# Three row-count arms of a mixture-of-experts loop: the smallest arm laid next in line and made to hold the whole expert, the larger ones set apart, and the expert's buffers made fixed tiles

## The chip, the cores and the metric

The kernel runs on one core of a Trainium2 chip. The metric is the device time of one execution in microseconds (us).

## What is computed

The program is two transformer blocks over 256 tokens of width 1024. The first block has a mixture-of-experts feed-forward layer: a router gives each token its best 4 of 32 experts, and each expert is a gate-up product, a clamped activation and a down product with its own weights. Cut to that layer, the reference is:

```python
def clamped_swiglu(hdn):
    x_glu = jnp.minimum(hdn[..., :D_EXPERT], SWIGLU_LIMIT)
    x_lin = jnp.clip(hdn[..., D_EXPERT:], -SWIGLU_LIMIT, SWIGLU_LIMIT)
    return x_glu * jax.nn.sigmoid(SWIGLU_ALPHA * x_glu) * (x_lin + 1)

def moe_ffn(h, w_router, b_router, w_gate_up, b_gate_up, w_down, b_down):
    ...
    logits = (xt @ w_router).astype(jnp.float32) + b_router.astype(jnp.float32)
    top_v, top_i = lax.top_k(logits, TOP_K)
    gates = jax.nn.softmax(top_v, axis=-1)
    ...
    counts = jnp.bincount(e_flat, length=N_EXPERTS)
    ...
```

Which expert gets how many rows is known only when the program runs. Everything is in float32.

## The kernel before

Attention, the norms and the router come first (until about 190 us). Then a Python loop writes out the 32 experts one after the other. Nothing loops at run time: each expert has its own instructions, and branches choose among them by its count of rows `n`.

**Three arms.** For each expert `by_rows` is called twice, once for the gate-up part (label `up{e}`) and once for the down part (label `down{e}`). Each call writes `If(n > 32)` with an inner `If(n > 64)`. Over 64 rows the `mid` arm runs (and in its gate-up part a further test, `If(n > 96)` at L1334, leads to `wide`), over 32 rows the `narrow` arm, else the `few` arm, which is the `Else` and so a jump's target. `few` works on 32 rows, `narrow` on 64, `mid` on 64 and then on 32 more. By the lines that ran, with these inputs experts 9, 13 and 20 take `mid`, 0, 3, 4, 6, 11, 12, 19 and 25 `narrow`, the other 21 `few`, and `wide` doesn't run. Each engine runs every branch for itself. L1317 is the test for 32 rows, L1318 that for 64. At the head of an arm a hint for TensorE (PE) names the branch that comes next (`down{e}` or `up{e+1}`) as likely taken.

**What stands around the arms.** Between the two parts stand `combine` (4 matmuls at L1052, which add the previous expert's output rows to the tokens) and `mask` for the next expert (VectorE, DVE). The down part also prepares the next expert: `gather` (L888) and `gather_out`, `slots` (L987, L989), `slots_out`, `turn_x` (L999). It ends with `rows_out`, a copy on ScalarE (ACT, L1044) and a subtract on DVE (L1047). The next expert's gate-up part begins with its bias, two matmuls at L1038 into the PSUM bank `gl`, which the activation of the expert before was read from by DVE. In the `few` arm the gate-up reads are at L1025 (`gate_up`), the turning of the hidden rows at L1093 (`few_T`), the down reads at L1103 (`few_out`).

**The weight stream.** An expert's weights are 12 slabs of 1024 KB, 8 for gate-up and 4 for down. The class `Stream` issues all of them in order on one queue, SyncE's (SP), at L192, into 17 slots of SBUF taken in turn (11 of a tile named `w`, 6 of tiles named `hi`, `hx`, `lo`, `lx`). When `W.done(i)` is called in the program, slab i's slot is handed to the slab 17 places on, whose load then waits, at run time, for PE's semaphore to show that the last read of slab i is done in whichever arm ran. The calls for slabs 0 to 7 of an expert stand after its `up{e}` branch, those for slabs 8 to 11 after its `down{e}` branch. SP's queue is in order: a load that waits holds up all behind it.

**Buffers.** `xT`, `dT` and `gs` of an expert come from a pool with two buffers, `eb`, `d` and `y` from one with one buffer.

Of the kernel before, what the change touches and what calls it, by code (L numbers as in the profile page):

```python
# [8 lines left out]
F32 = mybir.dt.float32  # L9
F32R = mybir.dt.float32r  # L10
# [9 lines left out]
T, D, NE, DFF = 256, 1024, 32, 2816  # L20
# [76 lines left out]
def kernel(tc, a, out, taps=None, stop=None):  # L97
# [3 lines left out]
    def P(n, bufs=1, stack=es, side="right", **k):  # L101
        return stack.enter_context(tc.tile_pool(name=n, bufs=bufs, side=side, **k))
# [778 lines left out]
    def mask_rows(d, t, e):  # L881
        nc.vector.tensor_scalar(d[:, t, :], C["iota2"], pos[:, t, e:e + 1], None, op0=OP.is_equal)
# [50 lines left out]
    pk0 = P("blk2a")  # L933
    ms = ExitStack()
    m1 = P("moe1", 1, ms)
    m2 = P("moe2", 2, ms)
    GN = {}

    def load_gn(i):
# [11 lines left out]

    acc = [two(t, True) for t in range(2)]

    PRE = {}

    def alloc(e):
        PRE[e] = (m2.tile([128, 4, 128], F32, name="xT"), m2.tile([128, 2, 128], F32R, name="dT"),
                  m1.tile([128, 3, 128], F32R, name="eb"), m2.tile([128, 1], F32, name="gs"))

    banks = {n: one(i) for i, n in enumerate(("ga", "gp", "gl", "li"))}  # L960

# [8 lines left out]
                                C["d32"][:, e:e + 1], None, op0=OP.mult)  # L970

    def mask(e):
        d = m1.tile([128, 2, 128], F32, name="d")
        for t in range(2):
            mask_rows(d, t, e)
        slab_rows(e)
        return d

    def gather_out(b):
        xe = m1.tile([128, 512], F32, name="xe")  # L980
# [68 lines left out]
    def combine(y, dT):  # L1049
        for t in range(2):  # L1050
            for hf in range(2):
                nc.tensor.matmul(acc[t][:, hf * 512:hf * 512 + 512], dT[:, t, :], y[:, hf, :], start=False,  # L1052
                                 stop=False, skip_group_check=True)

    def few_up(e):

        xT, dT, eb, gs = PRE[e]
        b = bank("gl")
        bias(b, eb[:, 1, :], 0)
        bias(b, eb[:, 2, :], 512, False)  # L1060
        nc.vector.tensor_copy(gs[32:64], gs[0:32])
        for o in (0, 64):
            nc.vector.tensor_copy(dT[o + 32:o + 64], dT[o:o + 32].bitcast(F32))
        for k in range(8):
            gate_up((b,), xT, W.get(MOE0 + 12 * e + k), k, 32)
# [41 lines left out]
    def narrow_up(e):  # L1107

        xT, eb = PRE[e][0], PRE[e][2][:, 0, :]
        gl, li = bank("gl"), bank("li")  # L1110
        bias(gl, eb, 0)
        bias(li, eb, 512)
        for k in range(8):
            gate_up((gl, li), xT, W.get(MOE0 + 12 * e + k), k, 64)
# [31 lines left out]
    def mid_up(e):  # L1146

        xT, (eb, *eg) = PRE[e][0], (PRE[e][2][:, q, :] for q in range(3))
        base = MOE0 + 12 * e
        d = m1.tile([128, 2, 128], F32, name="d")  # L1150
        for t in range(2):
            nc.vector.tensor_scalar(d[:, t, :], C["iota4"], pos[:, t, e:e + 1], None, op0=OP.is_equal)
        gl, li = bank("gl"), bank("li")
        bias(gl, eb, 0)
        bias(li, eb, 512)
        gx = bank("ga")
        for t in range(2):
            for q in range(4):
                nc.tensor.matmul(gx[32 * q:32 * q + 32, 0:256], d[:, t, 32 * q:32 * q + 32],
                                 h2[:, t, q * 256:q * 256 + 256], start=(t == 0), stop=(t == 1),  # L1160
                                 skip_group_check=True, tile_position=(0, 32 * q))
        gp = bank("gp")
        for t in range(2):
            nc.tensor.transpose(gp[:, t * 128:(t + 1) * 128], d[:, t, :], ident)
        for t in range(2):
            nc.tensor.matmul(gp[:, 256:257], d[:, t, :], gate[:, t, e:e + 1], start=(t == 0), stop=(t == 1),
                             skip_group_check=True)
        xe = m1.tile([128, 512], F32, name="xe")
        nc.scalar.activation(xe[:, 0:256], gx[:, 0:256], AF.Copy)
        nc.vector.tensor_copy(gs2, gp[:, 256:257])  # L1170
        for hf in range(2):
            nc.vector.tensor_scalar(dT2[:, hf], gp[:, 0:256].rearrange("p (t i) -> p t i", t=2),
                                    C["hm"][:, hf:hf + 1], None, op0=OP.mult)
        gate_up((gl, li), xT, W.get(base), 0, 64)
        gt = bank("ga")
        for c in range(2):
            nc.tensor.transpose(gt[:, c * 128:(c + 1) * 128], xe[:, c * 128:(c + 1) * 128], ident)
        xT2 = m1.tile([128, 2, 128], F32, name="xT2")
        nc.scalar.activation(xT2, gt[:, 0:256].rearrange("p (c s) -> p c s", c=2), AF.Copy)
        gate_up((gl, li), xT, W.get(base + 1), 1, 64)  # L1180
        b2 = bank("ga")
        bias(b2, eg[0], 0)
        bias(b2, eg[1], 512, False)
        for k in range(2, 10):
            if k < 8:
                gate_up((gl, li), xT, W.get(base + k), k, 64)
            gate_up((b2,), xT2, W.get(base + k - 2), k - 2, 32)
# [37 lines left out]
    def wide(e, c0):  # L1225

        base = MOE0 + 12 * e
        d = m1.tile([128, 2, 128], F32, name="d")
        pc = m1.tile([128, 2], F32, name="pc")
        sel = m1.tile([128, 2], F32R, name="sel")  # L1230
        nc.vector.tensor_scalar(pc, pos[:, :, e], float(-c0), None, op0=OP.add)
# [53 lines left out]
                    nc.tensor.matmul(acc[t][:, hf * 512:hf * 512 + 512], dT[:, t, :], y[:, q, :], start=False,  # L1285
                                     stop=False, skip_group_check=True)

    alloc(0)
    slab_rows(0)
    slots(0, d0, banks["gp"])  # L1290
    xe = gather_out(banks["ga"])
# [12 lines left out]
                nc.tensor.matmul(acc[t][:, HV[hf]], gT[:, t * 128:(t + 1) * 128], bd[:, HV[hf]], start=True,  # L1304
                                 stop=False, skip_group_check=True)

    y = None
    bias_down()
    W.done(BIAS)

    def by_rows(n, label, ahead, wide_too, mid, narrow, few):

        def hint():
            if ahead:
                tc.mark_branch_hint_location(ahead, "LikelyTaken", [mybir.EngineType.PE])

        with tc.If(n > 32, label=label) as cmp:  # L1317
            with tc.If(n > 64) as many:  # L1318
                hint()
                if wide_too:  # L1320
                    wide_too()
                mid()
            with many.Else():
                hint()
                narrow()
        with cmp.Else():
            hint()
            few()

    for e in range(NE):  # L1330
        n = nc.values_load(cnt[0:1, e:e + 1], min_val=0, max_val=T)  # L1331

        def more():
            with tc.If(n > 96):  # L1334
                wide(e, 96)
                with tc.If(n > 224):
                    wide(e, 224)

        by_rows(n, f"up{e}", f"down{e}", more, lambda: mid_up(e), lambda: narrow_up(e), lambda: few_up(e))
        for k in range(8):  # L1340
            W.done(MOE0 + 12 * e + k)
        if e:
            combine(y, PRE[e - 1][1])
        if e == 1:
            early_loads()
        d = None
        if e + 1 < NE:
            alloc(e + 1)
            d = mask(e + 1)
        y = m1.tile([128, 2, 512], F32R, name="y")  # L1350
        by_rows(n, f"down{e}", f"up{e + 1}" if e + 1 < NE else None, None, lambda: mid_down(e, d, y),
                lambda: narrow_down(e, d, y), lambda: few_down(e, d, y))
        for k in range(8, 12):
            W.done(MOE0 + 12 * e + k)
    combine(y, PRE[NE - 1][1])

    ms.close()
    rb_stack.close()
# [602 lines left out]
```

## Time and profile before

| | us |
|---|---|
| median of 3 runs | 2109.08 |
| lowest and highest of them | 2105.88 and 2111.14 |
| the profiled execution, its own time | 2107.37 |
| its span in the profile | 2105.6 |
| PE busy in the span | 1810.1 |
| DVE busy | 941.3 |
| ACT busy | 674.9 |

The span is what the profiler saw of the program; the profiled execution's own time is 1.77 us more. Busy times are sums over stages with different limits, so a share of the whole span says little about the expert stage, which lies between about 203 and 1225 us. The names PEld and PEq stand for PE's weight loads and PE's sequencer, the part that takes instructions, waits and branches.

### The profile page before, as it was taken

The numbers are of one execution on the slowest core, as the hardware profiler recorded it, in microseconds if no ns is written. First come the engines' busy times: TensorE is split into PE (matmuls) and PEld (weight loads), VectorE is DVE, ScalarE is ACT, GpSimd is POOL, SyncE is SP. The second block draws the span as 40 slices with busy tenths as digits, with TensorE's granted clock in tenths as the row PEclk, the third lists the DMA queues.
The fourth block names the chain that finished last, engine by engine and source line by source line (L and its number), as shares of the span: only waits on it lengthen the run. The fifth ranks groups of instructions, "written<-read, shape, count | busy, mean of one in ns | idle before, by whom it ended". The sixth has DMA issues, their size and how long they took to land.

```text
span 2105.6 us, 28938 instructions
## 1 busy us (share of the span) xinstructions
PE 1810.1 (86%) x11311; PEld 1160.3 (55%) x11311; DVE 941.3 (45%) x1687; ACT 674.9 (32%) x1149; POOL 365.5 (17%) x337
## 2 busy tenths in 40 slices
PE   7998878876878777877877778999999989999998
PEld 4775223322222222222212158998998778988996
DVE  3763222212112221122112159956576579665763
ACT  3452111101111111011101055544564456545752
POOL 3333000000000000000000034214352233132640
PEclk9997999988998998989878789999999999999999
DMA  9868999997986999899999954445455544453552
GB/s 399 344 250 303 404 413 415 414 412 322 399 326 259 410 413 415 348 388 413 413 414 413 398 173 135 142 175 185 151 182 212 179 132 142 169 194 136 179 195 87
DMA packets 102215, 603.00 MB, mean 286 GB/s; under 512 B 9888, under 2 KB 10576, under 8 KB 47024
## 3 DMA queue, kind: packets, MB, share of 16 engines
q1 hardware_dynamic: 97984, 586.72, 71.3%
q0 software_dynamic: 3952, 12.53, 1.9%
q8 instruction: 179, 2.93, 0.6%
q14 instruction: 100, 0.82, 0.1%
HBM read 598.13 MB, written 1.08 MB: 285 GB/s over the span
## 4 chain that ended last, share of the span: by engine, by line
issue 50%; PE 35%; DVE 9%; POOL 2%; ACT 2%; POOLq 1%; DMA 0%; DVEq 0%; SPq 0%; ACTq 0%
PE psum L354 11%; PE psum L353 10%; PE psum L352 10%; DVE lo L325 1%; DVE lx L325 1%; POOL v L245 1%; DVE gl L1732 1%; DVE gl L1516 1%; DVE h L577 1%; PE psum L1666 0%; DVE x L285 0%; PE psum L448 0%; POOLq L1331 0%; ACT hTh L357 0%; PE psum L416 0%
## 5 line engine op out<-in xcount | busy, mean ns | idle before, releaser
L1025 PE MATMUL psum<-w,xT 128*32 128x512 f32 (+1 forms) x1504 | 265.2, 682 | 26.1 <-DMA w<-in_wgu_dram 24.5
L354 PE MATMUL psum<-hTh,lo 128*128 128x256 f32 x848 | 240.6, 284 | 2.6 <-DVE lo L325 2.6
L352 PE MATMUL psum<-hTh,hi 128*128 128x256 f32 x848 | 242.2, 286 | 0.4 <-DVE yl L1536 0.4
L353 PE MATMUL psum<-hTl,hi 128*128 128x256 f32 x848 | 240.5, 284 | 0.0
L248 POOL TENSOR_TENSOR yr<-v,mhalf 128x1 f32<-128x1 f32 (+1 forms) x26 | 21.0, 808 | 1164.6 <-DVE v L245 1163.3
L325 DVE TENSOR_TENSOR lo<-w,hi 128x2048 fp32r<-128x2048 f32 x84 | 193.7, 2309 | 59.2 <-ACT hi L319 59.2
L319 ACT ACTIVATE hi<-w 128x2048 fp32r<-128x2048 f32 x93 | 177.6, 1913 | 86.4 <-PE psum L354 51.2
L1007 DVE TENSOR_SCALAR g<-psum 64x256 f32<-64x256 f32 (+1 forms) x70 | 29.3, 418 | 364.9 <-PE psum L1025 364.2
L1025 PEld LDWEIGHTS psum<-w,xT 128*32 128x32 f32 (+1 forms) x1504 | 64.5, 129 | 206.4 <-issue 143.4
L1008 ACT ACTIVATE s<-g 64x256 f32<-64x256 f32 (+1 forms) x70 | 28.8, 411 | 452.8 <-DVE g L1007 452.8
L352 PEld LDWEIGHTS psum<-hTh,hi 128*128 128x128 f32 x848 | 162.7, 192 | 3.7 <-issue 3.0
L354 PEld LDWEIGHTS psum<-hTh,lo 128*128 128x128 f32 x848 | 162.4, 192 | 2.8 <-DVE lo L325 2.8
L353 PEld LDWEIGHTS psum<-hTl,hi 128*128 128x128 f32 x848 | 162.4, 191 | 0.0
L1047 DVE TENSOR_TENSOR y<-psum,y 64x512 fp32r<-64x512 f32 x64 | 44.1, 689 | 209.5 <-ACTq L1317 124.5
L1778 POOL TENSOR_TENSOR cv<-cv,cv 128x256 f32<-128x256 f32 x44 | 86.3, 1960 | 135.5 <-ACT cv L1777 129.7
L1038 PE MATMUL psum<-bgh,eb 128*128 128x512 f32 x70 | 32.7, 557 | 87.0 <-issue 72.6
L354 PE MATMUL psum<-hTh,lx 128*128 128x256 f32 x368 | 104.1, 283 | 2.7 <-DVE lx L325 2.7
L352 PE MATMUL psum<-hTh,hx 128*128 128x256 f32 x368 | 104.4, 284 | 0.0
L325 DVE TENSOR_TENSOR lx<-w,hx 128x2048 fp32r<-128x2048 f32 x40 | 92.4, 2310 | 26.3 <-ACT hx L319 26.2
L353 PE MATMUL psum<-hTl,hx 128*128 128x256 f32 x368 | 103.9, 282 | 0.0
L888 PE MATMUL psum<-h,d 128*64 128x512 f32 x248 | 73.2, 700 | 35.3 <-DVE l L1010 16.5
L1772 DVE SCALAR_TENSOR_TENSOR cv<-psum,cols,cv 128x255 f32<-128x255 f32 x176 | 72.8, 475 | 62.3 <-ACT cv L1768 62.3
(427 smaller groups left out, 3774.3 us busy)
## 6 DMA issues: line engine op xcount, KB each, us to landing
w<-in_wgu_dram SPq DMA_DIRECT2D x169, 1024.0 KB, 19.8
w<-in_wpk_dram SPq DMA_DIRECT2D x168, 1024.0 KB, 5.0
w<-in_wd_dram SPq DMA_DIRECT2D x83, 1024.0 KB, 20.1
lo<-in_wgu_dram SPq DMA_DIRECT2D x29, 1024.0 KB, 20.1
hi<-in_wgu_dram SPq DMA_DIRECT2D x28, 1024.0 KB, 18.9
hi<-in_wd_dram SPq DMA_DIRECT2D x16, 1024.0 KB, 20.8
lo<-in_wd_dram SPq DMA_DIRECT2D x15, 1024.0 KB, 20.8
hx<-in_wgu_dram SPq DMA_DIRECT2D x15, 1024.0 KB, 20.1
```

The source lines that it names most:

```text
L319: nc.scalar.activation(s.his[i], W.get(i), AF.Copy)
L325: (eng or nc.vector).tensor_tensor(s.los[i], W.get(i), s.his[i].bitcast(F32), OP.subtract)
L352: nc.tensor.matmul(o, lh, rh, start=start, stop=False, **k)
L353: nc.tensor.matmul(o, lh, rl, start=False, stop=False, **k)
L354: nc.tensor.matmul(o, ll, rh, start=False, stop=stop, **k)
L888: nc.tensor.matmul(b[64 * j:64 * j + 64, :], d[:, t, 64 * j:64 * j + 64], h2[:, t, j * 512:j * 512 + 512], start=(t == 0), stop=(t == 1), ...
L1007: nc.vector.tensor_scalar(g, gl[:, c], 7.0, None, op0=OP.min)
L1025: nc.tensor.matmul(b[o:o + n, :], l, w[:, q * 512:q * 512 + 512], start=False, stop=(k == 7), skip_group_check=True, tile_position=(0, o))
L1038: nc.tensor.matmul(b, lhsT, bgh[:, o:o + 512], start=first, stop=False, skip_group_check=True)
L1047: nc.vector.tensor_tensor(y[o, hf, :], yb[r, :], y[r, hf, :].bitcast(F32), OP.subtract)
L1772: nc.vector.scalar_tensor_tensor(cv[q][:, o], bnk[:, q, i], c4[q][:, 2 * d:2 * d + 1], cv[q][:, o], op0=OP.mult, op1=OP.add)
L1778: nc.gpsimd.tensor_tensor(cv[0], cv[0], cv[1], OP.mult)
```

## The change

The test for 32 rows gets a flag that makes its false side, the `few` arm, the block that comes next in line (`preferred_fallthrough_block=False`), and the tests for 64 and 96 rows get the same flag. The `few` arm now holds the whole expert in the branch `up{e}`: gate-up, `combine` of the previous expert, `mask` for the next one, down part. The branch `down{e}` has no `Else` any more: an expert of at most 32 rows passes it by. `combine` and `mask` have gone from between the two branches into each arm. In the arms for more rows the gate-up part hints `down{e}`, and the down part `up{e+1}`; the `few` arm hints `up{e+1}`. The calls of `W.done` stay where they were, behind the two branches. `xT`, `dT`, `gs` become two fixed tiles each, taken in turn, and `EB`, `dm` and `Y` one fixed tile each, so the count of buffers is the same.

```diff
@@ -933,7 +933,6 @@
     pk0 = P("blk2a")
     ms = ExitStack()
     m1 = P("moe1", 1, ms)
-    m2 = P("moe2", 2, ms)
     GN = {}
 
     def load_gn(i):
@@ -951,11 +950,13 @@
 
     acc = [two(t, True) for t in range(2)]
 
-    PRE = {}
-
-    def alloc(e):
-        PRE[e] = (m2.tile([128, 4, 128], F32, name="xT"), m2.tile([128, 2, 128], F32R, name="dT"),
-                  m1.tile([128, 3, 128], F32R, name="eb"), m2.tile([128, 1], F32, name="gs"))
+
+    ROWS = [(m1.tile([128, 4, 128], F32, name=f"xT{i}"), m1.tile([128, 2, 128], F32R, name=f"dT{i}"),
+             m1.tile([128, 1], F32, name=f"gs{i}")) for i in range(2)]
+    EB = m1.tile([128, 3, 128], F32R, name="eb")
+    PRE = [(ROWS[e % 2][0], ROWS[e % 2][1], EB, ROWS[e % 2][2]) for e in range(NE)]
+    dm = m1.tile([128, 2, 128], F32, name="d")
+    Y = m1.tile([128, 2, 512], F32R, name="y")
 
     banks = {n: one(i) for i, n in enumerate(("ga", "gp", "gl", "li"))}
 
@@ -970,11 +971,9 @@
                                 C["d32"][:, e:e + 1], None, op0=OP.mult)
 
     def mask(e):
-        d = m1.tile([128, 2, 128], F32, name="d")
         for t in range(2):
-            mask_rows(d, t, e)
+            mask_rows(dm, t, e)
         slab_rows(e)
-        return d
 
     def gather_out(b):
         xe = m1.tile([128, 512], F32, name="xe")
@@ -1147,7 +1146,7 @@
 
         xT, (eb, *eg) = PRE[e][0], (PRE[e][2][:, q, :] for q in range(3))
         base = MOE0 + 12 * e
-        d = m1.tile([128, 2, 128], F32, name="d")
+        d = dm
         for t in range(2):
             nc.vector.tensor_scalar(d[:, t, :], C["iota4"], pos[:, t, e:e + 1], None, op0=OP.is_equal)
         gl, li = bank("gl"), bank("li")
@@ -1225,7 +1224,7 @@
     def wide(e, c0):
 
         base = MOE0 + 12 * e
-        d = m1.tile([128, 2, 128], F32, name="d")
+        d = dm
         pc = m1.tile([128, 2], F32, name="pc")
         sel = m1.tile([128, 2], F32R, name="sel")
         nc.vector.tensor_scalar(pc, pos[:, :, e], float(-c0), None, op0=OP.add)
@@ -1285,7 +1284,6 @@
                     nc.tensor.matmul(acc[t][:, hf * 512:hf * 512 + 512], dT[:, t, :], y[:, q, :], start=False,
                                      stop=False, skip_group_check=True)
 
-    alloc(0)
     slab_rows(0)
     slots(0, d0, banks["gp"])
     xe = gather_out(banks["ga"])
@@ -1304,55 +1302,62 @@
                 nc.tensor.matmul(acc[t][:, HV[hf]], gT[:, t * 128:(t + 1) * 128], bd[:, HV[hf]], start=True,
                                  stop=False, skip_group_check=True)
 
-    y = None
     bias_down()
     W.done(BIAS)
 
-    def by_rows(n, label, ahead, wide_too, mid, narrow, few):
-
-        def hint():
-            if ahead:
-                tc.mark_branch_hint_location(ahead, "LikelyTaken", [mybir.EngineType.PE])
-
-        with tc.If(n > 32, label=label) as cmp:
-            with tc.If(n > 64) as many:
-                hint()
-                if wide_too:
-                    wide_too()
+    def first_part(up, e):
+
+        up(e)
+        if e:
+            combine(Y, PRE[e - 1][1])
+        if e + 1 < NE:
+            mask(e + 1)
+
+    def second_part(down, e):
+        down(e, dm if e + 1 < NE else None, Y)
+
+    def arm(n, label, mid, narrow, few=None, ahead=None):
+
+        def hint(l):
+            if l:
+                tc.mark_branch_hint_location(l, "LikelyTaken", [mybir.EngineType.PE])
+
+        with tc.If(n > 32, label=label, preferred_fallthrough_block=False) as cmp:
+            with tc.If(n > 64, preferred_fallthrough_block=False) as many:
+                hint(ahead[0])
                 mid()
             with many.Else():
-                hint()
+                hint(ahead[0])
                 narrow()
-        with cmp.Else():
-            hint()
-            few()
+        if few:
+            with cmp.Else():
+                hint(ahead[1])
+                few()
 
     for e in range(NE):
         n = nc.values_load(cnt[0:1, e:e + 1], min_val=0, max_val=T)
-
-        def more():
-            with tc.If(n > 96):
+        after = f"up{e + 1}" if e + 1 < NE else None
+
+        def mid_first():
+            with tc.If(n > 96, preferred_fallthrough_block=False):
                 wide(e, 96)
                 with tc.If(n > 224):
                     wide(e, 224)
-
-        by_rows(n, f"up{e}", f"down{e}", more, lambda: mid_up(e), lambda: narrow_up(e), lambda: few_up(e))
+            first_part(mid_up, e)
+
+        def few():
+            first_part(few_up, e)
+            second_part(few_down, e)
+
+        arm(n, f"up{e}", mid_first, lambda: first_part(narrow_up, e), few, (f"down{e}", after))
         for k in range(8):
             W.done(MOE0 + 12 * e + k)
-        if e:
-            combine(y, PRE[e - 1][1])
         if e == 1:
             early_loads()
-        d = None
-        if e + 1 < NE:
-            alloc(e + 1)
-            d = mask(e + 1)
-        y = m1.tile([128, 2, 512], F32R, name="y")
-        by_rows(n, f"down{e}", f"up{e + 1}" if e + 1 < NE else None, None, lambda: mid_down(e, d, y),
-                lambda: narrow_down(e, d, y), lambda: few_down(e, d, y))
+        arm(n, f"down{e}", lambda: second_part(mid_down, e), lambda: second_part(narrow_down, e), None, (after, after))
         for k in range(8, 12):
             W.done(MOE0 + 12 * e + k)
-    combine(y, PRE[NE - 1][1])
+    combine(Y, PRE[NE - 1][1])
 
     ms.close()
     rb_stack.close()
```

## Rows read from the trace of the kernel before

**Rows 1.** The page: slices of the span, and the gate-up loads (issue to landing).

```profile
GB/s 399 344 250 303 404 413 415 414 412 322 399 326 259 410 413 415 348 388 413 413 414 413 398 173 135 142 175 185 151 182 212 179 132 142 169 194 136 179 195 87
...
w<-in_wgu_dram SPq DMA_DIRECT2D x169, 1024.0 KB, 19.8
```

**Rows 2.** Windows of the expert stage; last columns clock, DMA share, GB/s.

```profile
203.00:1205.00 1002.00, 787.21 (x4310) 260.66 (x4306) 219.62 (x574) 125.03 (x270) 0.00 (x0) 0.89 0.96 389
615.00:635.00 20.00, 15.87 (x84) 5.09 (x84) 3.19 (x9) 1.22 (x3) 0.00 (x0) 0.91 0.34 127
660.00:685.00 25.00, 19.65 (x124) 7.79 (x124) 4.04 (x11) 2.64 (x5) 0.00 (x0) 0.80 0.61 220
685.00:880.00 195.00, 152.01 (x860) 50.11 (x852) 43.10 (x114) 24.22 (x53) 0.00 (x0) 0.89 1.01 412
```

**Rows 3.** PE's waits in the expert stage: total us, times, longest.

```profile
PE psum L1038 <- issue: 72.6, 25, 5.1
...
PE psum L888 <- DVE l L1010: 16.5, 7, 3.2
PE psum L1038 <- PEq L1334: 14.4, 3, 5.5
```

**Rows 4.** PE's waits from expert 9 to the start of expert 14.

```profile
PE psum L1038 <- issue: 10.5, 4, 4.2
PE psum L1038 <- PEq L1334: 10.4, 2, 5.5
PE psum L888 <- issue: 7.3, 1, 7.3
```

**Rows 5.** PE's waits from expert 20 to the start of expert 22.

```profile
PE psum L1038 <- PEq L1334: 4.0, 1, 4.0
PE psum L1038 <- issue: 2.8, 1, 2.8
```

**Rows 6.** Branches at L1317: ns min/median/max.

```profile
L1317 DVEq COMPARE_BRANCH  x64: 43/56/60, 193.7 to 1182.9; - x64
L1317 PEldq COMPARE_BRANCH  x64: 74/600/6554, 194.1 to 1199.9; - x64
```

**Rows 7.** The same in the last six experts.

```profile
L1317 PEldq COMPARE_BRANCH  x12: 350/840/6235, 1025.7 to 1199.9; - x12
```

**Rows 8.** The test for 96 rows at L1334.

```profile
L1334 PEldq COMPARE_BRANCH  x3: 6187/6226/7053, 448.8 to 834.1; - x3
...
L1334 PEldq EVENT_SEMAPHORE  x3: 51/51/51, 455.0 to 840.3; - x3
```

**Rows 9.** Timeline of PE in expert 13, gate-up reads, first and last.

```profile
622.89 1.94 PE L1025 MATMUL psum<-w,xT 128*64 128x512 f32 x8
...
645.58 1.04 PE L1025 MATMUL psum<-hi,xT 128*32 128x512 f32 x8
```

**Rows 10.** Timeline of SP's loads, experts 13 and 14.

```profile
638.23 3.19 SPq L192 DMA_DIRECT2D w<-in_wgu_dram  x3
...
646.68 0.34 SPq L192 DMA_DIRECT2D hi<-in_wgu_dram  x1
...
674.78 0.89 SPq L192 DMA_DIRECT2D hx<-in_wgu_dram  x1
680.00 0.34 SPq L192 DMA_DIRECT2D lx<-in_wgu_dram  x1
...
686.27 2.27 SPq L192 DMA_DIRECT2D w<-in_wgu_dram  x1
```

**Rows 11.** Timeline of PE in expert 14.

```profile
676.85 1.22 PE L1038 MATMUL psum<-bgh,eb 128*128 128x512 f32 x2 [2.10 <-issue]
...
686.13 1.19 PE L1052 MATMUL psum<-y,dT 128*128 128x512 f32 x4
```

**Rows 12.** Timeline of ACT at the end of expert 14.

```profile
697.16 1.21 ACT L1044 ACTIVATE y<-psum 64x512 fp32r<-64x512 f32 x2 [2.07 <-PE psum L1103]
```

**Rows 13.** Timeline of DVE at the end of expert 14.

```profile
698.40 1.41 DVE L1047 TENSOR_TENSOR y<-psum,y 64x512 fp32r<-64x512 f32 x2 [5.91 <-ACTq L1317]
```

## The prediction, made before the changed kernel was run

> **What bounds the kernel now.** I read the slices of the page first, then windows over the expert stage, PE's waits in it, single branches, and last the order of loads and reads around one large expert.
>
> In the expert stage the DMA stands at 412 to 415 GB/s for most slices, and a load takes 19.8 us from issue to landing while a slab alone takes 1024 KB / 412 GB/s = 2.55 us: some eight loads share the wire, which is full [rows 1]. Twelve slabs are 30.5 us an expert, and in the stretch without a dip PE is busy 152 of 195 us and waits for slabs [rows 2]. A faster arm changes nothing there. Over 203 to 1205 us the mean is 389 GB/s [rows 2], so 1002 x (1 - 389/412) = 56 us is all that the stage can win. That loss lies in dips behind the experts with over 64 rows (9, 13, 20): the wire falls to 127 and 220 GB/s around expert 13 [rows 2]. There PE is late, all 17 slots are full, and the stream stands until PE has read. So there are two kinds of time: most of the stage, where PE's stalls are free, and the run-ups from expert 9 to the start of 14 and from 20 to the start of 22, where each us on PE is a us of the whole.
>
> PE's stalls of the stage sum high: 72.6 us of "issue" ahead of the bias and 14.4 us behind the test for 96 rows [rows 3]. Only the run-ups' part counts: 10.5 + 10.4 + 7.3 = 28.2 [rows 4] and 4.0 + 2.8 = 6.8 [rows 5], together **35.0 us**.
>
> **The change, part by part.**
>
> *The skip of `wide`.* PE's branch at L1334 took 6.2 us each time, and 14.4 us of it showed as idle time, 4.8 each, the rest being covered by work already queued [rows 3, 8]. With the false side in line this goes: -14.4.
>
> *The jump into `narrow`'s and `mid`'s arms.* By the flag the false side of the test for 64 rows comes next too. So `narrow` loses an unhinted jump: the 7.3 us of idle time ahead of a gather are one such fetch, in a run-up [rows 4]: -7.3. `mid` gains two unhinted jumps. That in its gate-up part stands where the skip of `wide` stood, just as close behind the start: 3 x 4.8 = +14.4. That in its down part stands ahead of a gather at which PE waits for DVE in any case, 16.5/7 = 2.4 us [rows 3]; an average shown stall is 72.6/25 = 2.9 us [rows 3], so 3 x (2.9 - 2.4) = +1.5. Bounds: nothing for either, if a jump is short enough to find its target loaded; 3 x 7.3 each if none is covered [rows 4].
>
> *Jumps out and back for more than 32 rows.* The jump out is hinted, and hinted branches in the last six experts mostly took 0.35 to 0.84 us [rows 7], inside the time PE's queue covers: 0. The jump back at the end of an arm has no hint. The down arm's is in the waits of before (the true arms jump over `few`, and the next start waited 2.10 us [rows 11]): these waits I leave as they are. The gate-up arm's was short of that: six experts of the run-ups (9, 11, 12, 13, 19, 20) by 2.9 less 2.4 of DVE's wait, 6 x 0.5 = +3.0. Bounds: 0 and 6 x 2.9 = 17.4.
>
> *`few` holding the whole expert.* PE loses the branches between its parts. They matter in one expert of the run-ups alone, 10, and hardly show there: 0. Before, hints reached the `few` jump; in line it needs none.
>
> *The new wait.* An engine that passes `down{e}` by must top up its semaphore for the work that it didn't do there, as at L1334 [rows 8], and it does so only when it comes to that branch, behind its own work. The next bias waits for DVE to have read its bank; DVE comes to the top-up behind ACT's copy and its own subtract at the end of `rows_out`, 1.21 + 1.41 = 2.6 us after PE's last matmul [rows 12, 13]. What is queued behind the bias is all gate-up reads, and so the slots. In the run-ups that is once (expert 10): +2.6; elsewhere slabs are late anyway. Bounds: 0 and 2.6.
>
> The run-ups then sum to -14.4 - 7.3 + 14.4 + 1.5 + 0 + 3.0 + 2.6 = **-0.2 us**: what it saves on the skip of `wide` it pays in other jumps.
>
> *Slots that come free later.* This is the part that I weigh most. A load waits for one value of PE's semaphore, whichever arm ran, so an arm's reads must lie at a fixed distance from its end. The rows show it: in expert 13 the gate-up reads run from 622.89 to 646.6 [rows 9], but its eight slots are handed on between 638.23 and 646.68, over the last reads, not as the first slabs are done [rows 10]. In `few` of expert 14 it is different: the reads begin at 678.0, behind the bias of 676.85 [rows 11], and the loads for their slots go out from 680.00 to 686.27, one after each slab [rows 10], because the gate-up reads are the last thing in that arm. In the changed kernel the arm goes on through `combine`, `gather`, `slots`, `turn_x` and the down part, while in the other arms the gate-up reads are still the last but `combine`. The value that means "slab 0 read" is then reached, in `few`, some thirty counted matmul groups before its end: slab 0's slot comes free only once `combine` is done, at 686.13 + 1.19 = 687.3 [rows 11], not at 680.0 [rows 10], 7.3 us later, and the next ones in the course of the gather and the down part.
>
> On a full wire with free slots ahead that costs nothing: later slabs are still waited for. It costs where `few` follows a long arm, as the wire is then empty: the last load before 680.00 goes out at 674.78 [rows 10], 5.2 us earlier, twice a slab's time, and the wire was down at 220 GB/s [rows 2]. So the stream starts 7.3 us later, less 2.1 us if the stall at the start of expert 14 goes [rows 11]: 5.2 to 7.3; I take 5.5, since loads already out cover little. That holds for experts 14 and 21 (behind 13 and 20): 11.0. Expert 10, behind 9, is followed by a run-up in which PE sets the time: 0. Expert 1 follows `narrow` with the stream just begun: 0 to 7.3, I take 4. Sum **+15.0 us**. What is queued behind the late load: all loads of the queue, in order, and so expert 15's and 22's reads. Bounds: 0 (the wire not yet empty, or slots counted otherwise) and 4 x 7.3 = 29.
>
> *Fixed tiles.* As many buffers as before, so no wait moves: 0. DVE's and ACT's branches take 0.06 us [rows 6], so what they gain or lose in branches is 0.
>
> Sum: 2107.4 (the profiled execution's own time) - 0.2 + 15.0 = **2122 us**. That execution lies 1.7 us below the median, inside the three runs, so I don't correct for it.
>
> [...] PE's branch at L1317 took from 0.07 to 6.55 us, DVE's 0.06 [rows 6]. [...]
>
> **The rivals.**
>
> *A: the run-ups' stalls all go* (the jump to `mid` lands in what is loaded or is covered, and the ways back too). 35.0 us go, the new wait brings 2.6, the late slots 15.0: 2107.4 - 17.4 = 2090 us. For it: all of these stalls are fetches, and hints work where they stand early [rows 7]. Against it: the way back and the test for 64 rows have none. It decides from the point where the run-ups lose over 15 us, about half their stalls.
>
> *B: no change.* The late slots cost nothing (or as much as the stalls save): 2107.4 - 0.2 = 2107 us, within 6. For it: the loads that the large expert's down part frees may bridge the gap. Against it: 220 GB/s [rows 2].
>
> *C: every jump out and back pays.* The six ways back of the gate-up arms at 2.9 in place of 0.5 (+14.4) and the three jumps into `mid`'s down arm at 2.9 in place of 0.5 (+7.2), on top of the forecast: 2122 + 22 = 2144 us. For it: 6.2 us three times out of three for an unhinted branch [rows 8].
>
> **How the numbers follow.** Forecast 0.44, A 0.27, B 0.14, C 0.15. A measurement of this kernel can tell 0.3%, about 6.3 us. The forecast's own range is 2112 to 2132: its terms with bounds, late slots from 5 to 25. The range for 8 in 10 reaches from A to just past C, 2089 to 2146; it leaves out half of A's lower side and C's upper. Faster is A, 0.27; the same is B and a little, 0.15; slower the rest, 0.58.
>
> **What would show it.** Right: in expert 14 the first load after 675 us goes out after `combine`, not after the first gate-up reads, and the dip behind experts 13 and 20 is longer; no branch of 6.2 us at L1334; PE's bias behind a `few` expert names DVE's or its sequencer's wait. Wrong: PE's idle time ahead of the bias in the run-ups falls far below 17 us without a new wait beside it (A), or the loads in expert 14 still go out one after each read slab (B).

## The result: slower by 8%, and the profile after

| | us |
|---|---|
| before, median of 4 runs | 2110.11 |
| after, median of 4 runs (2279.65 to 2290.55) | 2285.69 |
| ratio after to before | 1.0823, 95% interval 1.0796 to 1.0851 |

The forecast was 2122 us with a range of 2089 to 2146: the result lies 140 us above its upper end. The sign was right, the cause was not.

The page of the changed kernel, slices and loads, as in [rows 1] (the lines of the code have moved: the test for 32 rows is now L1325, that for 64 L1326, for 96 L1342, the bias L1037, the gate-up reads L1024, `combine` L1051, the down reads of `few` L1102, the sigmoid L1007):

```profile
GB/s 397 303 284 315 322 408 313 383 387 206 301 365 156 274 383 402 377 184 324 401 398 304 400 372 165 143 140 168 183 161 185 208 177 133 133 187 144 179 185 110
...
w<-in_wgu_dram SPq DMA_DIRECT2D x169, 1024.0 KB, 9.9
```

No slice reaches the 412 to 415 GB/s of a full wire any more, and a load lands in 9.9 us, not 19.8: by the 2.55 us of a slab some four are in flight, not eight. The window over the longer expert stage (last columns: clock, DMA share, GB/s), against 389 GB/s in [rows 2]:

```profile
203.00:1400.00 1197.00, 781.06 (x4353) 267.48 (x4352) 228.78 (x587) 179.36 (x318) 2.16 (x2) 0.82 0.83 328
```

PE's waits in that stage, as in [rows 3]:

```profile
PE psum L1037 <- issue: 294.4, 22, 26.0
PE psum L1102 <- ACT xT L999: 17.0, 20, 0.9
```

The idle time ahead of the bias has gone from 72.6 + 14.4 to 294.4 us, and of all PE's waits not one names a load of weights any more. Before, PE waited 38.8 us for weights in that stage, most of it in this line:

```profile
PE psum L1025 <- DMA w<-in_wgu_dram: 24.5, 22, 2.4
```

So the bound has changed over: the wire set the pace before, PE does now. It isn't that PE's own work takes longer: its granted clock in the stage fell from 0.89 to 0.82 of full speed, but it is busy 781.06 us there, and was 787.21 before [rows 2].

Where PE stands, one `few` expert (28) and the start of the next shows it, on PE's timeline:

```profile
1272.89 1.19 PE L1037 MATMUL psum<-bgh,eb 128*128 128x512 f32 x2 [11.82 <-issue]
...
1288.00 1.92 PE L1102 MATMUL psum<-w,xT 128*32 128x512 f32 x16 [0.85 <-ACT xT L999]
1289.86 0.34 PE L1092 MATMUL psum<-cst,h 64*128 64x64 f32 x2
1290.56 1.92 PE L1102 MATMUL psum<-w,xT 128*32 128x512 f32 x16 [0.37 <-ACT xT L1093]
1303.20 1.19 PE L1037 MATMUL psum<-bgh,eb 128*128 128x512 f32 x2 [10.72 <-issue]
```

The expert's work runs from 1272.89 to 1292.5, 19.6 us, and then PE stands still for 10.72 us. Its sequencer's branches in that gap (ns min/median/max) say why:

```profile
L1325 PEldq COMPARE_BRANCH  x4: 73/2718/6011, 1290.6 to 1302.9; - x4
```

and the one among them that lies between 1297 and 1302 us:

```profile
L1325 PEldq COMPARE_BRANCH  x1: 5358/5358/5358, 1297.0 to 1297.0; - x1
```

Two branches of 6.0 and 5.4 us, back to back, with 0.1 us for the other two. The order of the changed program's instructions tells what they are. `few` is next in line, but the arms for more rows lie in place behind it. At its end it jumps over all gate-up arms (302 PE instructions) to the test of the down part, finds itself at most 32 rows, and jumps over the down arms (97). Such counts, here and below, are of the program, a matmul with its weight load counted once; the trace has more records, for the 32 gate-up matmuls of an arm 64 matmuls and 64 weight loads. In every `few` expert of the trace there are these two, 5.9 to 7.4 and 3.7 to 8.0 us.

What comes in during a long branch, the trace shows too: instructions. The page counts what the instruction queue brought, before and after, in packets of 16 KB (2.93 MB / 179):

```profile
q8 instruction: 179, 2.93, 0.6%
q8 instruction: 201, 3.29, 0.6%
```

In the trace's records of that queue, each of the changed kernel's 63 branches of over 3 us in the expert stage has such a fetch beginning inside it, 51 have one and 12 have two, and the last of them begins 2.5 us (median) before the branch ends. None of the 82 branches under 0.7 us has one. The gap above has them at 1292.6 and 1294.2 us in the first branch and at 1299.8 in the second.

I took apart the stage by arm: the mean time on PE's sequencer from one expert's load of its count to the next's, for experts 1 to 30, with the sum, and beside it all that PE waited for weight loads.

| kernel | few (20) | narrow (7) | mid (3) | sum, us | PE's waits for weights, us |
|---|---|---|---|---|---|
| before | 26.0 | 33.5 | 65.2 | 950.6 | 38.8 |
| after | 32.6 | 38.2 | 71.5 | 1134.3 | 0 |

Of the 183.7 us more, `few` brings 132.0 (20 x 6.6), `narrow` 32.8, `mid` 18.9. The wire alone would take 30 x 30.5 = 915 us for these experts. PE's branches in the stage sum to 234 us before (42 of over 3 us) and 393 us after (63): 159 us of the difference.

### The profile page after: what moved, and what is told of

Same layout as the page of the kernel before. It is cut to its first block, busy times and chain, and to the rows that moved or that the text cites. A ratio compares the mean times of both kernels' runs of the same rounds, so it can differ in the third digit from the quotient of the medians.

```text
span 2285.6 us, 29219 instructions
## 1 busy us (share of the span) xinstructions
PE 1792.6 (78%) x11311; PEld 1162.4 (51%) x11311; DVE 946.1 (41%) x1687; ACT 722.3 (32%) x1186; POOL 364.1 (16%) x337
## 4 chain that ended last, share of the span: by engine, by line
issue 54%; PE 32%; DVE 9%; ACT 2%; POOL 2%; POOLq 1%; DVEq 0%; ACTq 0%
PE psum L354 10%; PE psum L353 9%; PE psum L352 9%; DVE lo L325 1%; DVE lx L325 1%; POOL v L245 1%; DVE gl L1737 1%; DVE h L577 1%; DVE gl L1521 1%; DVE ada_s L688 0%; PE psum L1671 0%; DVE x L285 0%; POOLq L1338 0%; PE psum L448 0%; ACT hTh L357 0%
## 5 line engine op out<-in xcount | busy, mean ns | idle before, releaser
L1037 PE MATMUL psum<-bgh,eb 128*128 128x512 f32 x70 | 37.7, 635 | 298.5 <-issue 294.4
L1024 PE MATMUL psum<-w,xT 128*32 128x512 f32 (+1 forms) x1504 | 257.3, 659 | 8.7 <-issue 8.7
L1007 ACT ACT_TABLE_LOAD x32 | 41.1, 1283 | 602.8 <-DVE g L1006 602.8
L1037 PEld LDWEIGHTS psum<-bgh,eb 128*128 128x128 f32 x70 | 16.4, 284 | 327.3 <-issue 326.7
L1024 PEld LDWEIGHTS psum<-w,xT 128*32 128x32 f32 (+1 forms) x1504 | 67.2, 129 | 181.7 <-issue 178.9
```

Of the source, the lines that this page charges most:

```text
L1007: nc.scalar.activation(s, g, AF.Sigmoid, scale=1.702)
L1024: nc.tensor.matmul(b[o:o + n, :], l, w[:, q * 512:q * 512 + 512], start=False, stop=(k == 7), skip_group_check=True, tile_position=(0, o))
L1037: nc.tensor.matmul(b, lhsT, bgh[:, o:o + 512], start=first, stop=False, skip_group_check=True)
```

## The experiments

Theory 1: the jumps that `few` must make over the arms behind it make PE slower than the wire. Rivals: late slots starve the wire (2), the ACT table load that the profile after shows 32 times (3), the hint fetches the wrong side (4). That a hint fetches, the traces show: the next fetch of 16 KB begins 3.2 us (before) and 3.0 us (after) behind it, in the median.

**One part alone: the flags, whole `few`, the tiles; and the hint taken away**

`flags_only`, an edit of the kernel before:

```diff
-        with tc.If(n > 32, label=label) as cmp:
-            with tc.If(n > 64) as many:
+        with tc.If(n > 32, label=label, preferred_fallthrough_block=False) as cmp:
+            with tc.If(n > 64, preferred_fallthrough_block=False) as many:
...
-            with tc.If(n > 96):
+            with tc.If(n > 96, preferred_fallthrough_block=False):
```

> The kernel before with the three flags alone; few still in two parts, each with its own branch. Theory 1 (the cost is the jumps that few must take, at its ends, over the large arms that lie behind it in place): each few expert still makes two such jumps, over the gate-up arms and over the down arms, 6.2 + 5.6 us as in the changed kernel, so an expert of at most 32 rows takes about 31 us and the whole 2270 to 2295 us. Rival 2 (few holding the whole expert frees its slots too late and the wire starves): slots are freed as before, so about 2107 us. Rival 3 (the table load on ACT that the changed kernel makes 32 times): no large effect if the loads are gone here.

Measured: 2201.51 us, ratio 1.0416 (1.0362 to 1.047). Half of the loss, with slots freed as before and the one table load of before: rival 2 alone is out, and so is theory 1's size. The two jumps are there (5.8 to 6.7, in the last expert 3.5, and mostly 3.3 to 6.2 us), but apart. PE's waits in the stage show what covers the first:

```profile
PE psum L1038 <- issue: 122.4, 22, 15.7
PE psum L1052 <- DVE l L1010: 55.5, 18, 4.1
```

The jump over the gate-up arms stands between gate-up and down part, where DVE and ACT work on the activation that PE needs next; `few` takes 28.5 us, `narrow` 39.5, `mid` 70.9: of the 109 us that experts 1 to 30 take more than before, `few` brings 50, and `narrow` and `mid` the rest. PE waits for no weights here either.

`whole_no_flags`, the changed kernel with the same three lines put back the other way:

> The changed kernel without the flags: few holds the whole expert, but the arms for more rows are next in line again and few is the hinted jump's target; hints and tiles as in the changed kernel. Theory 1: few's end lies next to the following branch, so the jump over the gate-up arms is made ahead, under a hint; left is the passing of the down arms, unhinted, about 5.5 us for each of 21 experts, which the wire hides: 2105 to 2135 us. Rival 2: the slots still come free late, so about 2285 us. My blind term for late slots was +15 us, 2122.

Measured: 2157.38 us, ratio 1.0232 (1.0203 to 1.026). Above my bounds: +47 us with `few` as the jump's target. PE waits 8.6 us for weights, `few` takes 27.6 us, and the 32 table loads are there. Each `mid` gate-up arm now ends on a branch of 5.9 to 6.0 us, which took 0.3 us in experts 9 and 13 before (4.25 in 20): `few`, holding the whole expert, has put the end of the branch farther away. But of the 48 us that experts 1 to 30 take more than before, `few` brings 32, `mid` 10 and `narrow` 7, and how `few`'s part divides among the table loads, the jump over the down arms (5.7 to 6.2 us in 8 of the 21) and its waits no run here shows.

`tiles_only`, the kernel before with the fixed tiles:

> The kernel before with the fixed tiles alone. Both theories: the same as before, 2105 to 2115 us. If it is over 2150, the tiles add a wait and all else has to be read again.

Measured: 2110.03 us, ratio 0.9993 (0.9975 to 1.001). As expected, the tiles are nothing.

`after_few_no_hint`, the changed kernel:

```diff
             with cmp.Else():
-                hint(ahead[1])
                 few()
```

> The changed kernel without the hint at the head of few. Theory 1: the jumps at few's ends have no hint either way, and the hint for the next expert's branch comes to nothing over two fetches, so 2280 to 2295 us, as in the changed kernel. Rival 4 (the hint fetches the wrong side and throws out what lies in line): several us less for each of 20 experts, 2180 to 2250 us.

Measured: 2270.79 us, ratio 1.0757 (1.0715 to 1.0799). The branch into the large arms, which that hint was for, took 5.2 to 5.5 us in eight of ten with it and without, so it helps nothing; it costs 15 us. That is below the 2280 to 2295 us of theory 1, which had it at nothing, and above the 2180 to 2250 of rival 4: a small part, not the cause.

**The jumps taken away, all of them or one of two**

`few_straight`, the changed kernel:

```diff
-        after = f"up{e + 1}" if e + 1 < NE else None
+        after = f"up{e + 1}" if e + 1 in (3, 4, 6, 9, 11, 12, 13, 19, 20, 25) else None
...
+        straight = e not in (0, 3, 4, 6, 9, 11, 12, 13, 19, 20, 25)
+        if straight:
+            few()
+        else:
+            arm(n, f"up{e}", mid_first, lambda: first_part(narrow_up, e), few, (f"down{e}", after))
-        arm(n, f"up{e}", mid_first, lambda: first_part(narrow_up, e), few, (f"down{e}", after))
...
+        if not straight:
+            arm(n, f"down{e}", ...)
-        arm(n, f"down{e}", ...)
```

> The changed kernel with the 21 experts that have at most 32 rows in these inputs written out straight, with no branch at all (valid for these inputs alone); the other 11 keep their branches, flags and hints as in the changed kernel. Theory 1 (the two jumps at the end of few, 12 us in each of 21 experts, are the loss, because they make PE slower than the wire): few falls from 31 to about 18 us, PE is ahead of the wire again, and the whole is at or below the kernel before: 2080 to 2120 us. Rival 2 (late slots, waits of the whole arm): over 2200 us, as the arm is still whole. What this can't tell apart is the ACT table load, which goes from few's experts too; table_early does that.

Measured: 2112.82 us, ratio 1.0004 (0.999 to 1.0019). All of the loss is gone with the branches of the 21 small experts, although `narrow` and `mid` are as in the changed kernel. Of the 63 branches of over 3 us 20 are left in the stage. (30 of the 32 table loads go with the branches; alone they are worth 26 us, as `table_early` shows below.) PE's waits show that the wire is the bound again (84.4 us for weights over all names):

```profile
PE psum L1024 <- DMA w<-in_wgu_dram: 52.4, 54, 1.9
PE psum L1037 <- issue: 43.4, 4, 15.9
```

That it isn't faster than before although no small expert branches any more fits the other side, that under the wire PE's stalls in the small experts were free, as the prediction had it. It doesn't prove it, as the larger arms, some of them slower here than before (expert 3 took 37.7 us, not 35.2), may have taken back a gain.

`one_jump`, the changed kernel with the down branch built for the 11 larger experts alone:

```diff
+        if e in (0, 3, 4, 6, 9, 11, 12, 13, 19, 20, 25):
+            arm(n, f"down{e}", ...)
-        arm(n, f"down{e}", ...)
```

> The changed kernel with the branch of the down part left out for the 21 experts that have at most 32 rows in these inputs (valid for these inputs alone). Each few expert then makes one unhinted jump, over the gate-up arms, in place of two. Theory 1 says the loss isn't the jumps' sum but what of them goes beyond the wire's 30.5 us an expert: with 18 to 20 us of work and one jump of 6 us few takes 25 to 27 us, under the wire, and most of the 173 us that few_straight won is won here too: 2115 to 2165 us. If each jump cost its time alone it would lie half way, near 2199.

Measured: 2195.97 us, ratio 1.0401 (1.0382 to 1.042). Half way, the answer that I had put against theory 1: each jump cost its time. By arm: `few` 27.0 us, `narrow` 36.5, `mid` 77.8, sum 1030.0. So `few` fell by 5.6 of 32.6 us, a whole jump, and is near the 26.0 of before; what is left of the loss lies mostly in `narrow` and `mid`. `mid` takes longer than even in the changed kernel: in experts 9 and 13 the two tests for 64 rows took 5.4 to 6.4 us, where they had taken 0.2 to 0.4. In the last experts, where `few` alone follows `few`, a jump does cost nothing: 27 to 30 take 30.7 to 30.9 us, the wire's time, with a jump of 5.9 to 6.2 us in them.

So as a rule for each expert by itself theory 1's threshold failed. That the 17 slots let PE average over several experts, so that it is PE's sum over the stage that has to stay under the wire's, is argued, not shown.

`after_no_wide`, the changed kernel without `wide` and its test:

```diff
-            with tc.If(n > 96, preferred_fallthrough_block=False):
-                wide(e, 96)
-                with tc.If(n > 224):
-                    wide(e, 224)
             first_part(mid_up, e)
```

> The changed kernel without the wide arm and its test for 96 rows, which doesn't run with these inputs (valid for these inputs alone). The skip of wide, 6.7 to 7.1 us in each of experts 9, 13 and 20, goes in full, and the jump at the end of few has some 170 PE instructions less to pass. Theory 1, with a jump that costs the same however far it goes once it is far: 2262 to 2272 us. If a jump gets cheaper with the distance: few's first jump falls below 6 us in all 21 and the whole below 2220 us.

Measured: 2211.0 us, ratio 1.0456 (1.0434 to 1.0477), 75 us less. That is more than the skip's 20 us, but not by the mechanism that I gave for it: `few`'s first jump passes 129 in place of 302 instructions and still takes 5.8 to 6.7 us (4.7 in the last expert). What got cheap is the end of `narrow`'s gate-up arm, which had to pass `wide` and `mid` (261 instructions, 5.8 to 7.1 us) and now passes `mid` alone (88), mostly for under 1 us: `narrow` falls from 38.2 to 33.0 us, `mid` from 71.5 to 66.5. That is 36 and 15 of the 76 us by which experts 1 to 30 get shorter; the other 25 are `few`'s, 32.6 to 31.4 us, half of it from jumps 0.3 us shorter each. The measured jumps over 97, 129, 261 and 302 instructions mostly took 5 to 7 us, whichever the count.

**The terms beside the jumps**

`table_early`, the changed kernel:

```diff
+    sg = m1.tile([128, 1], F32, name="sg")
+
     def first_part(up, e):
+        nc.scalar.activation(sg, C["hm"][:, 0:1], AF.Sigmoid)
         up(e)
```

> The changed kernel with a sigmoid on one column added at the head of each gate-up part, so that ACT loads its table there, while PE reads slabs, and not at the first sigmoid of the down part. If theory 1 is right that PE sets the pace of nearly every expert, what stands in its chain counts in full: 20 waits of 0.85 us for ACT ahead of the down reads and some 0.4 us for a few others, 15 to 30 us less than the changed kernel: 2255 to 2272 us. If the wire or the slots set the pace: 2280 to 2290, no change.

Measured: 2259.57 us, ratio 1.0705 (1.0682 to 1.0728), 26 us less. The changed kernel loads ACT's table in every expert, where the kernel before did so once in the stage; on ACT's lines of the changed kernel:

```profile
L1007 ACT ACT_TABLE_LOAD x32 | 41.1, 1283 | 602.8 <-DVE g L1006 602.8
```

With the added sigmoid none of these is left, and PE's 17.0 us ahead of the down reads have come down to 11.1, and other waits for the activation with them. `flags_only` had one load and `whole_no_flags` 32, so they come with holding the whole expert in one arm.

`whole_no_flags_pads`, `whole_no_flags` with:

```diff
+    def pad(up, e):
+        first_part(up, e)
+        for _ in range(32):
+            nc.tensor.matmul(banks["gp"][0:32, 0:1], ident[0:32, 0:32], ident[0:32, 0:1], start=True, stop=True,
+                             skip_group_check=True)
...
-            first_part(mid_up, e)
+            pad(mid_up, e)
...
-    first_part(narrow_up, e)
+    pad(narrow_up, e)
```

> whole_no_flags with 32 matmuls of one column put behind combine in the gate-up parts of narrow and mid. They change no result; by them the semaphore value at which a gate-up slot comes free is reached in few right behind the slab's read, not at the end of the arm. Their own cost is about 1.5 us in each of 11 experts. Blind theory (late slots cost 15 us): 2157 - 15 + some 6 = about 2148 us, and SP's loads no longer wait for combine. Theory 1 (PE sets the pace there too, slots late or not): 2155 to 2175 us, the pads' price.

Measured: 2242.88 us, ratio 1.0634 (1.0614 to 1.0654). Inconclusive as a price. The pads did what they were to do to the slots: SP's waits for `combine` fell from 116.5 us in 17 to

```profile
SPq L192 <- PE psum L1051: 7.7, 6, 1.6
```

but `narrow` rose from 34.4 to 44.7 us. The pads ran 24 us in all; the branch behind them, 5.5 to 7.3 us, lost the long matmuls that had covered it (PE's idle time ahead of the gather rose from 17.7 to 73.0 us).

`straight_late_slots`, `few_straight` with eight calls of `hold` in the straight experts:

```diff
+    LATE = []
+
+    def hold(*ks):
+        for k in ks if LATE else ():
+            w = W.get(MOE0 + 12 * LATE[0] + k)
+            nc.tensor.matmul(banks["li"][0:32, 400:401], w[:, 0:32], w[:, 0:1], start=True, stop=True,
+                             skip_group_check=True)
...
+            LATE.append(e)
+            few()
+            LATE.clear()
```

> few_straight with eight matmuls of one column in each of its 21 straight experts, one for each gate-up slab, put where the whole few arm lets go of that slab: behind combine, gather, slots, turn_x and the down reads. They change no result and hold the slots as late as the merged arm does, with no jump beside. In few_straight the wire sets the pace, so this prices late slots by themselves, against its ratio of 1.0004. My blind term: +15 us (bounds 0 and 29), ratio 1.007. Theory 1 says nothing on it in the changed kernel, where PE is behind anyway; if it is under 5 us here too, the term was wrong and not only hidden. The matmuls' own time, some 2 us in a few expert, lies under the wire.

Measured: 2125.24 us, ratio 1.0069 (1.0051 to 1.0087), 14 us above before and 12 above `few_straight`. This is the size of the blind term, in a kernel in which the wire sets the pace.

**Hints in the kernel before**

`narrow_hint`, the kernel before:

```diff
...
-            with tc.If(n > 64) as many:
-                hint()
+            with tc.If(n > 64, label=f"in_{label}") as many:
+                hint(ahead if label[0] == "d" else None)
...
             with many.Else():
-                hint()
+                hint(ahead if label[0] == "d" else f"in_{ahead}")
```

> The kernel before with other hints: the test for 64 rows gets a label, the gate-up arm of narrow hints that test of the down part (the jump it does take) in place of the test for 32 rows (which it doesn't take), and the gate-up arm of mid gives no hint. The unhinted jump into narrow's down arm took 5.2 to 6.0 us. In the run-ups there are three, so up to 7.3 + 2 x 3 us: 2095 to 2108 us if PE's stalls count there in full; the same as before if they are covered.

Measured: 2096.51 us, ratio 0.9943 (0.9927 to 0.996): faster than both kernels. PE's waits from expert 9 to the start of expert 14, against [rows 4]:

```profile
PE psum L1038 <- issue: 11.4, 4, 3.8
PE psum L1038 <- PEq L1334: 9.9, 2, 5.2
```

Experts 1 to 30 take 14 us less, `narrow` 32.2 us in place of 33.5. But the hint did its work in experts 3 and 19 alone, where the branch into `narrow`'s down arm fell from 6.0 to 0.4 us; in 0, 6, 11 and 12 it still took 5.0 to 5.5, and in 4 and 25 it had been short before. The 7.3 us ahead of a gather, now 1.2, were never that jump's. On PE's timeline of the kernel before they end at 492.18 us, in expert 9, a `mid` expert, in the middle of the gather of its down arm. No branch runs there; the trace has two fetches of 16 KB, at 483.7 and 489.7 us, behind the hint at the head of that arm. Why the second came so late is not shown.

`narrow_wide_hint`, the same with a label for the test for 96 rows and a second hint ahead of each hint for `up{e}`:

```diff
+            if l and l[:2] == "up":
+                tc.mark_branch_hint_location("w" + l[2:], "LikelyTaken", [mybir.EngineType.PE])
             if l:
                 tc.mark_branch_hint_location(l, "LikelyTaken", [mybir.EngineType.PE])
...
-            with tc.If(n > 96):
+            with tc.If(n > 96, label=f"w{e}"):
```

> The kernel narrow_hint with the test for 96 rows labelled as well and hinted in the down arms of the expert before, just ahead of the hint for the test for 32 rows. If both hints are kept, the 6.0 to 6.9 us at that test go in experts 9, 13 and 20: 2082 to 2092 us. If one hint drives out the other, the jumps to few or the skip stay unhinted: 2097 us or up to 15 us more.

Measured: 2118.22 us, ratio 1.0032 (1.0019 to 1.0045), some 20 us worse than `narrow_hint`. The branch at the test for 96 rows did get shorter, 6038/6122/6870 ns before the second hint and now

```profile
L1336 PEldq COMPARE_BRANCH  x3: 2102/3976/4989, 471.9 to 847.7; - x3
```

but at the test for 32 rows the median went from 530 ns to

```profile
L1319 PEldq COMPARE_BRANCH  x64: 73/2294/7068, 194.3 to 1209.0; - x64
```

By these two lines and the time, the second hint made the one test's branches shorter (median 6122 to 3976 ns) and the other's longer.

## Why the prediction was wrong, point by point

- **`few` holding the whole expert, costed at 0: the step that failed.** I wrote that in line `few` needs no jump. It needs none to enter (0.07 to 0.09 us at the test in line), and two to leave, because the flag changes which block is next and not where the others lie. I had left the place of the other arms open and priced only the ways back of the large arms. Measured: 5.9 to 7.4 and 3.7 to 8.0 us in each of 21 experts, back to back; 132 us over 20 experts.
- **"PE's stalls are free outside of the run-ups": at best right at the size of before, wrong at the size after.** `few_straight` fits it, as it gains nothing over the kernel before. But I never asked how much slack there was. The slack is the wire's 915 us less PE's own need. An estimate from the table: before, PE itself needed some 950.6 - 38.8 = 912 us, about as much as the wire, so there was next to none, and 12 us more in each of 20 experts go through it. With that the run-ups, on which the whole sum was built, stop being a part of the stage apart.
- **The skip of `wide`, -14.4.** Not gained. False comes next in line there too, but what lies there is one jump over `wide`. L1342 shows two branches an expert in place of one, the largest 7.1 us:

```profile
L1342 PEldq COMPARE_BRANCH  x6: 72/3386/7063, 516.6 to 973.2; - x6
```

- **The jumps into `narrow`'s and `mid`'s arms, -7.3, +14.4 and +1.5.** The -7.3 was read from the wrong place: the stall stands inside expert 9's `mid` down arm, as said under `narrow_hint`, and is no jump into `narrow`'s arm. The two tests that `mid` was to pay for took 0.2 and 0.3 to 0.4 us. That nothing came of the +14.4 either, so that it still cancels the -14.4 above, is luck.
- **The hinted jump out, 0.** It took 5.2 to 5.5 us in eight of ten large experts, with the hint and without it. Why the hint comes to nothing there (other fetches lie between it and the branch, in expert 2 of the changed kernel at 291.5, 293.7 and 299.3 us) is argued, not shown.
- **The ways back, +3.0.** Too small: the end of `narrow`'s gate-up arm alone took 5.8 to 7.1 us, and in `after_no_wide`, where it is cheap, `narrow`'s sum falls by 36 us.
- **Late slots, +15.0.** The mechanism and the size were right: `straight_late_slots` measured 12 to 14 us (there with slots late in all 21 small experts, where I had counted three), and in expert 14 of the changed kernel the first gate-up slot is handed on as forecast. `combine` on PE's timeline:

```profile
778.25 1.20 PE L1051 MATMUL psum<-y,dT 128*128 128x512 f32 x4
```

and SP's loads after the run-up, against [rows 10]:

```profile
769.89 0.33 SPq L192 DMA_DIRECT2D hx<-in_wgu_dram  x1
779.48 0.34 SPq L192 DMA_DIRECT2D lx<-in_wgu_dram  x1
```

The load goes out at 779.48, when `combine` ends at 779.45, 9.6 us after the one ahead of it and not 5.2. But it shows nothing in the time there, for PE waited for no weights at all. A right term was counted in a kernel whose bound it doesn't touch.
- **The new wait, +2.6.** It doesn't show. PE waits for DVE ahead of a bias once, 4.1 us, but in expert 4, behind a `narrow` expert; behind `few` the longer jumps would cover it.
- **What was missing:** ACT's table load in each expert, 26 us, which nothing in the trace of before showed.
- **Rival C** had the right idea, that each jump out and back costs a long branch, and 2144 us, since it counted the large arms' jumps in the run-ups and not `few`'s. In the changed kernel's trace each of the 63 long branches has a 16 KB fetch in it.

The parts don't add: flags +91, whole `few` +47, both +176. In `flags_only` the first of `few`'s jumps runs beside the activation; held in one arm, both jumps stand at its end, where nothing is left to run beside them. That the 38 us between are this is argued from the waits shown above.

## What to carry to other kernels

Laying the frequent arm next in line brought its jump in down to 0.07 to 0.09 us here and cost it two jumps out over the arms that lie behind, of 5.9 to 7.4 and 3.7 to 8.0 us; ask where the other blocks go, and count the ends of an arm as well as its start. "Stalls of this engine are free here" has a size: sum the engine's own need over the whole stage against the bound's, before and after, and only then say which stalls count (here some 912 us against 915 before, 1134 after). When a change crosses that line, terms worked out for the old bound (here the slots) drop out, however right they are.

## What the runs showed of the hardware that I had not expected

A long branch on PE has a fetch of instructions in it: in the traces of the kernel before and of the changed kernel each of the 42 and 63 branches of over 3 us in the stage has a 16 KB packet of the instruction queue beginning in it. The unhinted jumps over 97, 129, 261 and 302 instructions took mostly 5 to 7 us, at most 8.0. Those over 72 and 88 were mostly cheap (0.3 us for the former in two experts of three, mostly under 1 us for the latter in `after_no_wide`), but the count isn't all of it: in the kernel before, `narrow`'s jump over 62 instructions into its down arm took 5.2 to 6.0 us in six of eight experts, with that arm's hint spent on a branch that wasn't taken, and in `one_jump` the one over `narrow`'s gate-up arm alone, 41 instructions, 5.4 and 5.8 us in two experts of three.

With the hint at the jump that is taken, `narrow`'s branch fell from 6.0 to 0.4 us in two experts of eight (`narrow_hint`, -0.57% in all, part of it from elsewhere). Hints also cost: `few`'s hint for the next test, which wasn't taken after 14 of the 20 experts that give it, cost 15 us, and a second hint beside the first some 20. ACT's table, loaded once in the stage with the activations of the small expert spread over two branches, was loaded 32 times, 1283 ns each, with the whole expert in one arm.
